# Low halves of the weights in three feed-forward stages: a negated copy and an adding transfer in place of a VectorE subtraction

## The chip, the cores and the metric

The kernel runs on one core of a Trainium2 chip. The metric is device time in microseconds of one execution. A core has TensorE (PE, matrix products into PSUM), VectorE (DVE), ScalarE (ACT), GpSimd (POOL) and SyncE (SP), which run side by side and wait for each other through semaphores, each through its own instructions in order. Sixteen DMA engines move data between memory (HBM) and the on-chip SBUF. Here SP issues the loads.

## What is computed

Two layers of a diffusion transformer on 256 latent and 256 context tokens of width 1024. Each layer is a half feed-forward step (FFN), a mixer (attention in the first layer, an mLSTM in the second) and another half FFN, each with a modulation and a layer norm:

```python
def half_ffn(h, shift, scale, gate, w_in, w_out, g, b):
    xm = modulate(h, shift, scale)
    a, u = jnp.split(xm @ w_in, 2, axis=-1)
    y = (jax.nn.silu(a) * u) @ w_out
    return post_norm(h, 0.5 * gate * y, g, b)

for i in range(DEPTH):
    mod_lat = split((silu(c) @ ada_w[i] + ada_b[i]), N_MOD)
    ...
    h_lat = half_ffn(h_lat, ..., ffn_w_in[i, 0], ffn_w_out[i, 0], ...)
    ...
    o_lat, o_ctx = attention_mixer(...)   # or mlstm_mixer
    ...
    h_lat = half_ffn(h_lat, ..., ffn_w_in[i, 1], ffn_w_out[i, 1], ...)
```

`w_in` is 1024 x 5632, `w_out` 2816 x 1024, all in float32. The result is `h_lat`. The last FFN sees the latent tokens alone.

## The kernel before

Every float32 matrix product is made of three products in a rounded format, float32r: an operand x is split into a high part h (x rounded) and a low part l = x - h, also rounded, and `mm3` (line 207) adds Wh·Xh, Wh·Xl and Wl·Xh in PSUM (lines 211, 214, 215). So each weight has to be loaded, rounded and subtracted before TensorE can use it. Weights come in blocks of 128 x 1024 (512 KB), eight 128 x 128 tiles each. One block feeds 24 matmuls.

The way of one block is `chunk` (line 187). `raw` issues the load from SP's queue into one of three raw buffers (tag "raw", `RAW = 3`). `pair` takes one of seven buffers (tag "w", `WB = 7`), each of which holds a high and a low part. `split` has ScalarE write the high part (line 194) and VectorE the low part (line 199). Once VectorE has read the raw buffer, SP may load into it again; once TensorE has used both parts, the pair is free. `fine` cuts VectorE's subtraction into four quarters around the layer norms, so that the norm's steps can go in between.

`ffn` is called three times (layer 0 before and after the attention, and layer 1 before the mLSTM; the first, second and third FFN below). Each goes over the hidden width in two halves of 11 units. A unit (`unit_in`) multiplies two blocks of `w_in` with the 512 tokens, takes the SiLU of one result on ScalarE, multiplies it with the other on VectorE and splits the product. `unit_out` then adds the half's part of `w_out`, eight columns from 11 blocks. In the second and third FFN the first four units (`LEAD`), and in all three the last four columns (`TAIL`), run once for the latent and once for the context tokens at half width, with their blocks kept, so that the layer norm of one group of tokens runs under the products of the other. The first FFN begins with `start`, which has its own loads and does the first four units with code of its own. `ffn_last`, the attention and the mLSTM use `chunk`, too.

Beside the weights each of the three FFNs loads blocks of `ada_w` (56, 40 and 32 of 512 KB, tag "ada", two buffers) through the same queue, two or three after each unit. VectorE takes two dot products of each (line 290).

In which order each engine's instructions stand is decided when the program is built, by a scheduler that follows the order of the code and its own estimate of when operands are ready; a few instructions are held in program order. In the layer norm (`norm`) POOL adds up three squares (line 417) and subtracts in four tiles (line 454).

Of the kernel before, what the change touches and what calls it, by code (L numbers as in the profile page):

```python
# [13 lines left out]
AF = mybir.ActivationFunctionType  # L14
ALU = mybir.AluOpType
# [96 lines left out]
class Stream:  # L112


    def __init__(self, b, chunks, sh=0):
        self.b, self.chunks, self.kept = b, chunks, (None, None)
        self.sh = sh if callable(sh) else lambda c: sh
# [24 lines left out]
class Body:  # L142
    def __init__(self, ctx, tc, a, out):
        self.tc, self.nc, self.a, self.out = tc, tc.nc, a, out
        self.n = 0
        self.sp = ctx.enter_context(tc.tile_pool(name="sp", bufs=1))
        self.pp = ctx.enter_context(tc.tile_pool(name="pp", bufs=1, space=PSUM))
        self.later, self.running = [], []
        self.fence = {}
        self.fine = False  # L150

        self.nraw, self.spare = 0, None

# [33 lines left out]
    def chunk(self, src, sh=0):  # L187
        r = self.raw(src)
        h, l = self.pair(sh=sh)
        self.split(r, h, l)  # L190
        return h, l

    def split(self, x, h, l):
# [331 lines left out]
    def ffn(self, layer, s, gate, groups, side, start=None):  # L525
        nc, V = self.nc, self.nc.vector
        li = layer * 2 + s
        allg = BOTH
        call = lambda *k: side.get(k, lambda: None)()
        with self.tc.tile_pool(name=f"ffn{li}", bufs=1) as gp:  # L530
            self.gp, self.gt, self.gw, self.gn = gp, {}, T, NFH
            done = 0
            if start:
                start(self)
                done = NSTART

            def unit_in(j, w, g, steps={}):
                n = g[1] - g[0]
                pa, pu = self.mm(), self.mm()
                for k in range(ND):  # L540
                    for part, o in ((0, pa), (1, pu)):
                        self.mm3(o[:, :n], w(k * 2 + part), self.x(k, g), k == 0, k == ND - 1)
                    self.steps(steps.get((j, k), ""))
                self.ffn_g(j, pa, pu, g)

            def unit_out(hf, d, w, g, steps={}):
                t0, t1 = g
                y = self.mm()
                for i in range(NFH):
                    gh, gl = self.gt[hf * NFH + i]  # L550
                    self.mm3(y[:, : t1 - t0], w(d * NFH + i), (gh[:, t0:t1], gl[:, t0:t1]), i == 0, i == NFH - 1)
                    self.steps(steps.get((int(g == CTX), d - (ND - TAIL), i), ""))
                for gg in groups:
                    if gg[0] >= t0 and gg[1] <= t1:
                        v = 0 if gg[0] == 0 else 1
                        z = self.h[:, d, gg[0] : gg[1]]
                        V.scalar_tensor_tensor(z, y[:, gg[0] - t0 : gg[1] - t0], gate()[:, v, d : d + 1], z, ALU.mult, ALU.add)  # L557
                        if hf:
                            self.add_sum(gg, d)

            w_in, w_out = self.a["ffn_in"][li], self.a["ffn_out"][li]
            stream = lambda j: Stream(self, [w_in[2 * j + i] for i in range(2)])
            for hf in range(2):
                js = list(range(hf * NFH, (hf + 1) * NFH))[0 if hf else done :]
                if hf == 0 and not start:
                    first = js[:LEAD]
                    ws = {j: Keep(self, [w_in[2 * j + i] for i in range(2)], SH) for j in first}
                    for g in groups:
                        assert len(self.running) == (g == LAT)
                        for j in first:  # L570
                            unit_in(j, ws[j], g, LEADSTEP if g == LAT else {})
                    for j in first:
                        call("in", j)
                    js = js[LEAD:]
                for j in js:
                    unit_in(j, stream(j), allg)
                    assert not self.running
                    if j >= LEAD + FAFTER:
                        self.fine = False
                    call("in", j)  # L580
                    self.residual(2)
                if not hf:
                    self.residual(len(self.later))
                w = Stream(self, [w_out[hf * NFH + i] for i in range(NFH)])
                body = ND - TAIL if hf else ND
                for d in range(body):
                    unit_out(hf, d, w, allg)
                    call("out", hf, d)
                if body < ND:
                    w = Keep(self, w.chunks, SH, w)  # L590
                    self.fine = True
                    for g in groups:
                        for d in range(body, ND):
                            unit_out(hf, d, w, g, TAILSTEP)
                    self.steps(ENDSTEP)


    def ffn_last(self, layer, gate):
# [800 lines left out]
```

## Time and profile before

| What | Value |
|---|---|
| Time of two runs | 1698.13 and 1702.44 us, median 1700.29 |
| Span of the profiled execution, from the first to the last instruction (its time, with what lies around the span, is not given apart from the two above) | 1693.6 us |
| Instructions | 24765 |
| q1, the queue of the loads | 71072 packets, 248.15 MB, 43.1% of 16 engines' span |
| Mean rate of all DMA | 148 GB/s |
| Loads of `ffn_in` / `ffn_out` / `ada_w`, 512 KB each | 168 / 66 / 139 |

A row of a group gives the line, the engine, the operation, the tile written and the tiles read with their shape, and the count; then the busy time and the mean of one in nanoseconds; then the idle time of the engine just before, and what ended it. A wait row gives who waited for whom: the total in microseconds, how often, and the longest. A row of the timeline begins with its start and its duration in microseconds. DMA share is the mean busy share of the 16 DMA engines. The lines themselves stand in the prediction, where they are used.

### The profile page before, as it was taken

The numbers are of one execution on the slowest core, as the hardware profiler recorded it, in microseconds if no ns is written. First come the engines' busy times: TensorE is split into PE (matmuls) and PEld (weight loads), VectorE is DVE, ScalarE is ACT, GpSimd is POOL, SyncE is SP. The second block draws the span as 40 slices with busy tenths as digits, with TensorE's granted clock in tenths as the row PEclk, the third lists the DMA queues.
The fourth block names the chain that finished last, engine by engine and source line by source line (L and its number), as shares of the span: only waits on it lengthen the run. The fifth ranks groups of instructions, "written<-read, shape, count | busy, mean of one in ns | idle before, by whom it ended". The sixth has DMA issues, their size and how long they took to land.

```text
span 1693.6 us, 24765 instructions
## 1 busy us (share of the span) xinstructions
PE 1643.8 (97%) x9432; PEld 1441.6 (85%) x9432; DVE 1231.7 (73%) x2681; ACT 656.3 (39%) x1125; POOL 93.6 (6%) x114
## 2 busy tenths in 40 slices
PE   7999999999899999999999999999999999999997
PEld 6888888899887898888888998888889878999986
DVE  6799977659988899996334977643335967998687
ACT  5622133215465452212331543213322645556541
POOL 0000000002321100000000100000001001120000
PEclk9999999999999999999999999999999999999999
DMA  9576765412102346774222257642221232337542
GB/s 356 184 230 231 236 210 199 149 62 77 61 2 82 119 136 234 229 244 152 93 94 75 101 179 247 215 144 98 99 100 63 94 125 76 113 125 246 178 168 94
DMA packets 71910, 250.49 MB, mean 148 GB/s; under 512 B 7920, under 2 KB 10480, under 8 KB 71792
## 3 DMA queue, kind: packets, MB, share of 16 engines
q1 hardware_dynamic: 71072, 248.15, 43.1%
q8 instruction: 74, 1.21, 0.3%
q10 hardware_dynamic: 720, 0.76, 0.1%
q14 instruction: 44, 0.36, 0.1%
HBM read 247.83 MB, written 1.05 MB: 147 GB/s over the span
## 4 chain that ended last, share of the span: by engine, by line
PE 83%; DVE 11%; ACT 3%; DMA 2%; issue 1%; POOL 0%; ACTq 0%; DVEq 0%; SPq 0%
PE t L214 23%; PE t L215 23%; PE t L211 23%; PE t L668 4%; DVE t L199 3%; PE t L1165 2%; PE t L726 2%; PE t L728 2%; PE t L727 2%; ACT t L194 1%; PE t L380 1%; DVE t L473 1%; DVE t L400 1%; DVE t L475 1%; DVE t L1201 1%
## 5 line engine op out<-in xcount | busy, mean ns | idle before, releaser
L211 PE MATMUL t<-t,t 128*128 128x512 f32 (+2 forms) x2540 | 856.1, 339 | 10.1 <-ACT t L194 7.5
L214 PE MATMUL t<-t,t 128*128 128x512 f32 (+2 forms) x2540 | 858.5, 339 | 1.8 <-DVE t L475 1.3
L215 PE MATMUL t<-t,t 128*128 128x512 f32 (+2 forms) x2540 | 854.4, 337 | 1.9 <-DVE t L199 1.9
L199 DVE TENSOR_TENSOR t<-t,t 128x256 fp32r<-128x256 f32 (+2 forms) x793 | 494.8, 659 | 196.4 <-ACT t L194 195.8
L194 ACT CAST t<-t 128x1024 fp32r<-128x1024 f32 (+2 forms) x463 | 397.7, 880 | 587.0 <-PE t L215 311.2
L211 PEld LDWEIGHTS t<-t,t 128*128 128x128 f32 x2540 | 476.6, 188 | 65.7 <-ACT t L194 9.8
L214 PEld LDWEIGHTS t<-t,t 128*128 128x128 f32 x2540 | 477.7, 188 | 56.5 <-DVE t L475 2.5
L215 PEld LDWEIGHTS t<-t,t 128*128 128x128 f32 x2540 | 477.5, 188 | 55.3 <-DVE t L199 2.8
L290 DVE SCALAR_TENSOR_TENSOR t<-t,t 128x1024 bf16<-128x1024 f32 x224 | 262.6, 1220 | 15.9 <-DMA t<-in_ada_w 15.4
L522 DVE TENSOR_TENSOR t<-t,t 128x512 f32<-128x512 f32 (+1 forms) x93 | 54.0, 585 | 112.1 <-PE t L215 92.4
L521 ACT ACTIVATE t<-t 128x512 f32<-128x512 f32 (+1 forms) x93 | 47.4, 515 | 196.9 <-PE t L215 195.0
L417 POOL TENSOR_TENSOR t<-t,t 128x256 f32<-128x256 f32 x30 | 23.3, 777 | 1161.4 <-ACT t L407 1159.9
L557 DVE SCALAR_TENSOR_TENSOR t<-t,t,t 128x256 f32<-128x256 f32 x96 | 42.7, 478 | 54.2 <-PE t L215 54.2
L726 PE MATMUL t<-t,t 128*128 128x256 f32 (+1 forms) x256 | 80.4, 316 | 0.0
L728 PE MATMUL t<-t,t 128*128 128x256 f32 (+1 forms) x256 | 79.7, 314 | 0.0
L727 PE MATMUL t<-t,t 128*128 128x256 f32 (+1 forms) x256 | 79.5, 313 | 0.0
L1165 PE MATMUL t<-t,t 128*128 128x512 f32 (+1 forms) x248 | 54.8, 373 | 11.0 <-ACT t L274 5.2
L1165 PEld LDWEIGHTS t<-t,t 128*128 128x128 f32 x248 | 46.4, 220 | 19.0 <-ACT t L274 5.2
L668 PE MATMUL t<-t,t 128*128 128x512 f32 x264 | 60.0, 389 | 0.0
L668 PEld LDWEIGHTS t<-t,t 128*128 128x128 f32 x264 | 49.5, 188 | 10.2
L407 ACT ACTIVATE t<-t 128x256 f32<-128x256 f32 x72 | 26.1, 413 | 68.3 <-DVE t L400 68.3
L726 PEld LDWEIGHTS t<-t,t 128*128 128x128 f32 x256 | 49.6, 194 | 3.1 <-DVE t L789 0.3
(164 smaller groups left out, 1067.6 us busy)
## 6 DMA issues: line engine op xcount, KB each, us to landing
t<-in_ffn_in SPq DMA_DIRECT2D x168, 512.0 KB, 4.0
t<-in_ada_w SPq DMA_DIRECT2D x139, 512.0 KB, 4.2
t<-in_ffn_out SPq DMA_DIRECT2D x66, 512.0 KB, 3.7
t<-in_ffn_last SPq DMA_DIRECT2D x22, 512.0 KB, 3.7
t<-in_att_in SPq DMA_DIRECT2D x12, 512.0 KB, 3.5
t<-in_att_out SPq DMA_DIRECT2D x8, 512.0 KB, 3.9
t<-in_ml_qk SPq DMA_DIRECT2D x8, 512.0 KB, 3.4
t<-in_ml_v SPq DMA_DIRECT2D x8, 512.0 KB, 4.0
```

Source lines behind the costliest of these rows:

```text
L194: self.behind(self.nc.scalar.copy(h, x))
L199: self.behind(self.nc.vector.tensor_tensor(out=ls, in0=xs, in1=hs.bitcast(F32), op=ALU.subtract))
L211: ins = mm(out, wh, xh, start=first, stop=False)
L214: mm(out, wh, xl, start=False, stop=False)
L215: mm(out, wl, xh, start=False, stop=last)
L290: ins = nc.vector.scalar_tensor_tensor(self.tmp().bitcast(BF16), r, 1.0, self.cb[:, v, :], ALU.mult, ALU.mult, accum_out=to)
L522: V.tensor_tensor(out=sl, in0=sl, in1=pu[:, :n], op=ALU.mult)
L668: pin(nc.tensor.matmul(ys[tt][i], gs[g], ws[k][w][:, i * 512 : (i + 1) * 512], start=k == 0 and g == w == 0, stop=k == NF - 1 and g == 1,))
L726: mm(o, self.xh[:, k, c], wh, start=k == 0, stop=False)
L727: mm(o, self.xh[:, k, c], wl, start=False, stop=False)
L728: mm(o, self.xl[:, k, c], wh, start=False, stop=k == ND - 1)
L1165: mm = lambda *k, **kw: pin(nc.tensor.matmul(*k, **kw))
```

## The change

While a flag is set, from the start of the FFN's units to its end, in each of the three FFNs, `chunk` no longer calls `split`. ScalarE writes the high part as before, and then the negative of the rounded block into the low part's place. A DMA that POOL issues adds the raw block onto it: l = -h + x. The subtraction on VectorE, and its quarters, are gone for these blocks. The loads, the products and the buffers are the same. The attention, the mLSTM, `start`, `ffn_last` and all splits of activations still use `split`.

```diff
@@ class Body, __init__
         self.fine = False
+        self.added = False
@@ def chunk
         r = self.raw(src)
         h, l = self.pair(sh=sh)
-        self.split(r, h, l)
+        if self.added:
+            S = self.nc.scalar
+            self.behind(S.copy(h, r))
+            self.behind(S.activation(l, r, AF.Copy, scale=-1.0))
+            self.nc.gpsimd.dma_start(l, r, accum_op=ALU.add)
+        else:
+            self.split(r, h, l)
         return h, l
@@ def ffn
                 start(self)
                 done = NSTART
 
+            self.added = True
+
             def unit_in(j, w, g, steps={}):
...
                     self.steps(ENDSTEP)
+            self.added = False
```

The lines move by up to ten: in the changed kernel the high part is line 193, the negated copy 194, the adding transfer 195, and `split`'s two steps are 201 and 206.

What moves, first on ScalarE in the units of the second half of the first FFN (128x1024 rows are weight blocks, 128x512 rows the SiLU and the split of its product). Before:

```order
L194 CAST t_1885<-t_1883 128x1024
L521 ACTIVATE t_1676<-t_1614 128x512
L194 CAST t_1935<-t_1933 128x1024
L194 CAST t_1674<-t_1676 128x512
L194 CAST t_1964<-t_1962 128x1024
L521 ACTIVATE t_1755<-t_1693 128x512
```

and now:

```order
L528 ACTIVATE t_1703<-t_1639 128x512
L193 CAST t_1968<-t_1966 128x1024
L201 CAST t_1701<-t_1703 128x512
L194 ACTIVATE t_1968<-t_1966 128x1024
L193 CAST t_1998<-t_1996 128x1024
L194 ACTIVATE t_1998<-t_1996 128x1024
L528 ACTIVATE t_1784<-t_1720 128x512
```

Each weight block now has two rows, and a unit's SiLU (line 528, before 521) stands behind four passes over blocks where there were two.

SP's queue in the second products of the first half of the first FFN (line 180 or 179: weights; 291 or 284: `ada_w`). Before:

```order
L179 DMA t_1171<-in_ffn_out 128x1024
L284 DMA t_810<-in_ada_w 128x1024
L179 DMA t_1200<-in_ffn_out 128x1024
L284 DMA t_817<-in_ada_w 128x1024
L284 DMA t_892<-in_ada_w 128x1024
```

and now:

```order
L180 DMA t_1185<-in_ffn_out 128x1024
L291 DMA t_816<-in_ada_w 128x1024
L180 DMA t_1215<-in_ffn_out 128x1024
L291 DMA t_823<-in_ada_w 128x1024
L291 DMA t_900<-in_ada_w 128x1024
```

The interleaving stays, three `ada_w` loads to two weight loads; what a weight load waits for is now the transfer of the third block before it.

POOL between the second and the third FFN (lines 417 and 454, now 424 and 461, are the layer norm's; `t_8769` and the later transfers belong to the third FFN's first units). Before:

```order
L417 TENSOR_TENSOR t_8392<-t_8387,t_8390 128x256
L417 TENSOR_TENSOR t_8392<-t_8392,t_8395 128x256
L417 TENSOR_TENSOR t_8392<-t_8392,t_8399 128x256
L454 TENSOR_TENSOR t_66<-t_66,t_8496 128x256 x4
L417 TENSOR_TENSOR t_8691<-t_8686,t_8689 128x256
```

and now:

```order
L195 DMA t_8769<-t_8767 128x1024
L424 TENSOR_TENSOR t_8446<-t_8441,t_8444 128x256
L424 TENSOR_TENSOR t_8446<-t_8446,t_8449 128x256
L424 TENSOR_TENSOR t_8446<-t_8446,t_8453 128x256
L195 DMA t_8799<-t_8797 128x1024
L195 DMA t_8859<-t_8857 128x1024
L461 TENSOR_TENSOR t_66<-t_66,t_8548 128x256 x4
L195 DMA t_8889<-t_8887 128x1024
```

POOL's queue in an FFN was empty up to the norm; now the norm's rows stand between the triggers of transfers, each of which waits for ScalarE.

## The prediction

> **What bounds the kernel now.** I read the page's head first, then a table of the span cut into stretches, then the groups of instructions by form, and then the waits of the DMA queue. The head says that TensorE is the busy engine:
>
> ```profile
> span 1693.6 us, 24765 instructions
> PE 1643.8 (97%) x9432; PEld 1441.6 (85%) x9432; DVE 1231.7 (73%) x2681; ACT 656.3 (39%) x1125; POOL 93.6 (6%) x114
> ```
>
> The stretches (PE, PEld, DVE, ACT, POOL busy, granted clock, share of the 16 DMA engines, GB/s) show where. 36 to 369 us is the first FFN behind its start, 610 to 928 the second, 965 to 1296 the third; the short ones are the passages between stages.
>
> ```profile
> core 0: us, PE busy (x) PEld busy (x) DVE busy (x) ACT busy (x) POOL busy (x), PEclk, DMA share, GB/s
> 0.00:36.00 36.00, 24.96 (x102) 21.53 (x103) 19.40 (x41) 17.48 (x33) 0.19 (x4) 1.00 0.95 370
> 36.00:100.00 64.00, 64.00 (x300) 53.48 (x299) 54.79 (x87) 35.09 (x58) 0.00 (x0) 1.00 0.61 200
> 100.00:200.00 100.00, 100.00 (x443) 82.81 (x442) 95.18 (x158) 25.09 (x28) 0.00 (x0) 1.00 0.72 238
> 200.00:300.00 100.00, 100.00 (x442) 82.79 (x442) 79.42 (x126) 28.13 (x35) 0.00 (x0) 1.00 0.59 203
> 300.00:369.00 69.00, 69.00 (x356) 59.24 (x355) 37.24 (x78) 14.73 (x17) 0.00 (x0) 1.00 0.34 115
> 369.00:402.00 33.00, 31.63 (x262) 30.99 (x262) 29.80 (x86) 14.89 (x31) 8.04 (x10) 1.00 0.18 59
> 570.00:610.00 40.00, 36.69 (x295) 35.18 (x295) 37.79 (x115) 18.10 (x42) 5.54 (x7) 1.00 0.16 54
> 610.00:850.00 240.00, 240.00 (x1148) 202.15 (x1148) 183.82 (x310) 72.79 (x97) 0.00 (x0) 1.00 0.56 186
> 850.00:928.00 78.00, 78.00 (x396) 66.69 (x395) 28.91 (x58) 17.09 (x20) 0.00 (x0) 1.00 0.25 88
> 928.00:965.00 37.00, 34.90 (x291) 34.07 (x291) 32.99 (x101) 15.54 (x31) 8.05 (x10) 1.00 0.26 92
> 965.00:1100.00 135.00, 135.00 (x737) 117.22 (x736) 96.09 (x186) 50.54 (x82) 0.00 (x0) 1.00 0.61 205
> 1100.00:1296.00 196.00, 196.00 (x917) 164.43 (x916) 74.83 (x115) 48.09 (x56) 0.00 (x0) 1.00 0.30 105
> 1296.00:1333.00 37.00, 35.21 (x292) 34.37 (x292) 33.83 (x104) 18.60 (x37) 8.05 (x10) 1.00 0.20 66
> ```
>
> Inside the three FFNs TensorE is busy in every microsecond. VectorE, from which work is taken, reaches 95.18 of 100 us and still nothing waits for it. So no VectorE time that is freed there can shorten the span. What can be gained lies in the four passages, where TensorE idles 1.37, 3.31, 2.10 and 1.79 us, 8.6 us in all. The reader should also see the DMA column: 0.61, 0.72, 0.59 in the first FFN. That is what the change adds to.
>
> TensorE's pace, from its timeline, at full and at half width of the moving tile:
>
> ```profile
> 65.64 0.39 PE L211 MATMUL t<-t,t 128*128 128x512 f32 x1
> 65.87 0.39 PE L214 MATMUL t<-t,t 128*128 128x512 f32 x1
> ```
>
> ```profile
> 937.75 0.28 PE L211 MATMUL t<-t,t 128*128 128x256 f32 x1
> 937.87 0.28 PE L214 MATMUL t<-t,t 128*128 128x256 f32 x1
> ```
>
> A weight block of 128x1024 feeds 24 matmuls: 24 x 0.227 = 5.44 us at full width, 24 x 0.118 = 2.83 us for one pass at half width (the first four units and the last four columns of an FFN). ScalarE's timeline shows the same beat, one block in 5.44 us, and the first block of the first FFN split at 58.07 us for a matmul at 65.64:
>
> ```profile
> 58.07 1.98 ACT L194 CAST t<-t 128x1024 fp32r<-128x1024 f32 x2
> 103.97 1.05 ACT L194 CAST t<-t 128x1024 fp32r<-128x1024 f32 x1
> 109.41 1.05 ACT L194 CAST t<-t 128x1024 fp32r<-128x1024 f32 x1 [3.34 <-PE t L215]
> ```
>
> **What the change removes and adds on the engines.** The prices per block:
>
> ```profile
> L194 ACT CAST t<-t 128x1024 fp32r<-128x1024 f32 x310 | 325.2, 1051 | 520.4 <-PE t L215 307.9 <-issue 139.8 <-DVE t L660 24.7
> L290 DVE SCALAR_TENSOR_TENSOR t<-t,t 128x1024 bf16<-128x1024 f32 x224 | 262.6, 1220 | 15.9 <-DMA t<-in_ada_w 15.4
> L199 DVE TENSOR_TENSOR t<-t,t 128x1024 fp32r<-128x1024 f32 x200 | 243.6, 1222 | 132.5 <-ACT t L194 132.3
> ```
>
> 190 blocks go through it: 36 + 44 + 44 of the first products, 22 in each of three second products. VectorE loses 190 x 1.22 = 232 us, all under a busy TensorE: 0 us of span in the bodies. ScalarE gains a second pass of the same size. No row shows a scaled copy of a whole block; the cast of the same shape is nearest, 1.05 us, so 190 x 1.05 = 200 us. Its share in 100:200 goes from 25 to 25 + 100 x 1.05/5.44 = 44%: hidden, too, and the SiLU behind it waits 1 us at most. In the passages VectorE's low parts stood among the steps of the layer norm; I give that 2 of the 8.6 idle us (bounds 0 and 8.6).
>
> **The transfer that adds.** It is the term that decides, and no row shows such a transfer. It moves 190 x 0.524 = 100 MB. Its engine time is bounded by loads. From the row 100:200: 0.72 x 100 us for 23.8 MB, 45.4 blocks, is 1.59 us of all 16 engines per block; from 0:36, where the engines are full, 0.95 x 36 us for 25.4 blocks is 1.35 us. The lower end is one full-rate load, 1.35 us; the upper end three loads at the dearer price (read the block, read the low tile, write it), 4.8 us. I take two full-rate loads, 2.7 us: with two operands the reading doubles while reading and writing go side by side, as in a load, and where it matters the engines are full as in 0:36. The page "Collectives: The Full Stack" of the Trainium skill, in "The bandwidth ceiling", puts the cost of an adding transfer in its two source reads and gives 62.28 against 32.35 GB/s; by that ratio of 1.93 a block would take 2.6 us and the sum below come to about 1745. No run here shows it yet.
>
> Now per stage, all loads at 1.35 us. The fullest row with the weights' three buffers and the two of `ada` is 0.72, the start's is 0.95; I let the engines fill to 0.92, nearer to the second, since here something is always queued.
> - First FFN, 36 to 369: 12.8 + 23.8 + 20.3 + 7.9 = 64.8 MB, 124 blocks, 167 us; 58 additions, 157 us; 324/0.92 = 352 us in a stretch of 333: +19. Its last block is due a half-width pass (44 x 3 x 0.118 = 15 us) before the end: +15. Nothing absorbs it, since TensorE takes the first block 7.6 us after its split begins, and no store of finished blocks exists yet. +34.
> - Second FFN, 610 to 850: 186 GB/s x 240 us is 85 blocks, 115 us; 44 additions, 119; 254 us after the fill: +14. In the last 78 us it fits. Up to six finished blocks (6 x 5.44 = 33 us) can stand ahead; the half-width passes at its head drain them, so I let half be absorbed: +7.
> - Third FFN, 965 to 1100: 53 blocks, 72 us; 25 additions, 68; 151 us: +16, half of it +8. Then 0.30 leaves room.
>
> **The three raw buffers.** The load of block n+3 waits until the raw buffer of block n is free:
>
> ```profile
> SPq L179 <- DVE t L199: 1105.5, 289, 84.6
> SPq L284 <- DVE t L290: 240.6, 120, 4.0
> ```
>
> Now it is freed by the adding transfer. SP is one queue in order, so the `ada` loads behind a waiting weight load wait as well, and VectorE's dot products with them. Landing times, in the window 100 to 200 us and over the whole run:
>
> ```profile
> t<-in_ffn_out SPq DMA_DIRECT2D x11, 512.0 KB, 4.6
> ```
>
> ```profile
> t<-in_ffn_in SPq DMA_DIRECT2D x168, 512.0 KB, 4.0
> ```
>
> One turn of a buffer is 4.6 (load) + 0.6 (ScalarE busy) + 2.1 (two passes) + L, and three turns' worth of TensorE is 3 x 5.44 = 16.3 us; so L, from ScalarE's end to the landing, may be 9.0 us. I estimate L as 2.7 + (4.0 - 1.35) + about 1.1 us for POOL to issue = 6.5 (bounds 4.0, a load's landing, and 12, two landings of 4.6 and three more): a turn of 13.8, 4.6 us per block. That holds 5.44 but not the 2.83 of the half-width passes. At the head of the second and the third FFN three loaded blocks are followed by three at 4.6: 3 x 1.8 = 5 us, of which some store is left; 4 us each, +8. POOL's layer-norm steps now stand behind such triggers:
>
> ```profile
> 941.88 3.45 POOL L454 TENSOR_TENSOR t<-t,t 128x256 f32<-128x256 f32 x4 [7.96 <-DVE t L449]
> ```
>
> POOL waits 7.96 us there for VectorE anyway, and triggers that stand ahead wait only for ScalarE: 0.
>
> **The sum:** 34 + 7 + 8 + 8 - 2 = +55 us on a span of 1693.6. The two timed runs lie 4.5 and 8.8 us over that span, their median 6.7; I add 55 to the median, 1700.3: 1755 us.
>
> **The rivals.**
> - *Hidden anyway (not slower).* If an addition costs the engines less than (318 x 0.92 - 167)/58 = 2.2 us, the first FFN fits too; at 1.35 us and L = 4.0 a turn is 11.3 of 16.3 us. Then only the passages speak: about 1698. For it: SBUF at both ends, no row at all against it. Against: two operands.
> - *A dear addition.* At 4.8 us: first FFN 167 + 278 = 445/0.92 = 484 + 15, +166; second (98 blocks, 58 additions) 132 + 278 = 410/0.92 = 446 against 318, +128; third (92 blocks, 61 additions) 124 + 293 = 417/0.92 = 453 against 331, +122; less two stores of 33, +6 of passages: about 2055. The steps between give 143 us for each us of price, so 1920 stands for 3.85 us.
> - *Latency, not rate.* If L exceeds 9.0 us though the engines have room (POOL slow to issue, or late to land), the three buffers set the pace: L = 12 makes 6.43 us per block, +0.99 x 177 blocks, less two stores of 33: about 1810. VectorE could do it by holding up POOL, each step of 1.22 us. The page "SBUF — State Buffer" of the Trainium skill, in "Who interferes with whom", has VectorE's two-input steps take only the read side of a port shared with POOL, while writing descriptors needs the write side; by that this cause falls away, and no run here shows it.
>
> **How the numbers follow.** Engines too full at about two loads per addition: 0.50 (own range 1720 to 1830). Hidden: 0.27. Dear: 0.13. Latency: 0.10. The prediction is the first one's, 1755. The range 1695 to 1920 takes in hidden and latency, and leaves out the dear case beyond 3.85 us and a little below, some 0.15. A measurement of this kernel tells about 2%, 34 us, from no change. Slower: 0.9 of the first, dear and latency, 0.66 with a little off for a short latency. Same: the rest of the first and nearly all of hidden, 0.32. Faster would take 34 us where 8.6 are idle: 0.02.
>
> **What would show it.** DVE's busy time near 1000 and ACT's near 855 us; POOL's transfers of 512 KB landing in about 6.5 us; a DMA share above 0.9 from 100 to 300 us; TensorE waiting at L222 (the third product, of low parts) for the adding transfer, mostly in the first FFN; SP's loads waiting for that transfer, no longer for VectorE. It is wrong if the share stays under 0.9 and TensorE still never idles (hidden), if the second and third FFN lose as much as the first (dear), or if blocks come late while the engines have room (latency).

## The result, and the profile after

The changed kernel takes 1778.31 us (median of 2 runs, 1775.22 to 1781.39), against 1700.29 before: a ratio of 1.0468, 95% interval 1.0440 to 1.0496. It is slower, by 78 us. The profiled execution took 1781.39 us; 86.0 us of span separate it from the one of before (1779.6 against 1693.6). That is 8 us more than the medians differ by. Where both are given, a time is 1.7 to 2.3 us above its span, so the profiled execution of before took an estimated 1695 to 1696 us, less than either of its timed runs, and the one of after is the slower of its two; the stage lengths below contain this spread.

The page's head and its strip of the DMA engines in 40 slices (9 is 90% busy or more), then its rows of queues (packets, MB, share of the time of all 16 engines):

```profile
span 1779.6 us, 25229 instructions
PE 1668.4 (94%) x9432; PEld 1457.6 (82%) x9432; DVE 1014.8 (57%) x2362; ACT 832.7 (47%) x1315; POOL 256.8 (14%) x304
...
DMA  9799999972201949999998559999987232255552
...
q1 hardware_dynamic: 71072, 248.15, 40.2%
q0 software_dynamic: 27360, 99.63, 30.3%
```

VectorE lost 217 us of work, ScalarE gained 176, and neither is what counts. TensorE runs the same 9432 matmuls and is busy 24.6 us longer: some of them ran at a lower clock. The queue q0 carries the 190 adding transfers: 0.303 x 1779.6 / 190 = 2.84 us of all 16 engines each. The 248.15 MB of q1 are 473 blocks of 512 KB: 0.402 x 1779.6 / 473 = 1.51 us for a load.

Where the span grew shows in POOL's timeline, where the first sum of a layer norm marks the end of each stage. Before (first FFN, attention, second FFN, third FFN):

```profile
372.24 2.46 POOL L417 TENSOR_TENSOR t<-t,t 128x256 f32<-128x256 f32 x3 [371.81 <-ACT t L407]
567.54 2.40 POOL L417 TENSOR_TENSOR t<-t,t 128x256 f32<-128x256 f32 x3 [42.73 <-ACT t L407]
...
931.23 0.76 POOL L417 TENSOR_TENSOR t<-t,t 128x256 f32<-128x256 f32 x1 [337.35 <-ACT t L407]
...
1299.11 2.46 POOL L417 TENSOR_TENSOR t<-t,t 128x256 f32<-128x256 f32 x3 [340.09 <-ACT t L407]
```

and after:

```profile
403.77 2.45 POOL L424 TENSOR_TENSOR t<-t,t 128x256 f32<-128x256 f32 x3 [19.42 <-ACT t L414]
598.32 2.40 POOL L424 TENSOR_TENSOR t<-t,t 128x256 f32<-128x256 f32 x3 [3.96 <-ACT t L414]
989.23 2.45 POOL L424 TENSOR_TENSOR t<-t,t 128x256 f32<-128x256 f32 x3 [14.88 <-ACT t L414]
1384.88 2.45 POOL L424 TENSOR_TENSOR t<-t,t 128x256 f32<-128x256 f32 x3 [20.32 <-ACT t L414]
```

So the first FFN is 31.5 us longer, the attention 0.8 shorter, the second FFN 27.2 and the third 27.8 longer, and all behind them is unchanged: 31.5 - 0.8 + 27.2 + 27.8 = 85.7 of the 86.0. The three stages that the diff touches lose nearly alike, which the prediction didn't expect.

A table by stage (columns as in the prediction's) divides this further. Before:

```profile
66.00:372.20 306.20, 306.20 (x1414) 256.08 (x1413) 242.28 (x405) 84.47 (x103) 0.00 (x0) 1.00 0.57 192
567.50:931.20 363.70, 360.39 (x1883) 309.61 (x1882) 255.28 (x495) 111.63 (x166) 7.78 (x10) 1.00 0.44 148
931.20:1299.10 367.90, 365.80 (x1940) 315.61 (x1940) 203.84 (x399) 114.18 (x169) 8.05 (x10) 1.00 0.41 141
```

and after:

```profile
66.00:403.80 337.80, 312.62 (x1419) 258.86 (x1418) 180.25 (x335) 136.41 (x161) 48.16 (x57) 0.96 0.96 265
598.30:989.20 390.90, 367.34 (x1882) 314.39 (x1881) 183.34 (x380) 172.10 (x230) 62.38 (x74) 0.97 0.88 228
989.20:1384.90 395.70, 375.23 (x1941) 322.58 (x1940) 128.14 (x280) 174.91 (x234) 63.35 (x76) 0.97 0.85 217
```

Two things are to be seen. TensorE idles 25.2, 23.6 and 20.5 us in the three stages, where it idled 0, 3.3 and 2.1; and its busy time for the same work grew by 6.4, 7.0 and 9.4. And the DMA share, 0.57, 0.44 and 0.41 before, is 0.96, 0.88 and 0.85. In the first FFN 0.96 x 337.8 = 324 us of engine time stand against 306 us of matmuls: no order of the loads within the stage can hide that, as long as each takes this engine time. In the second and third it is 344 and 336 us, against 364 and 368 of before: over the whole stage it would fit.

What TensorE waits for (sum, times, longest), and what SP's queue, ScalarE and VectorE wait for:

```profile
PE t L218 <- ACT t L201: 44.4, 12, 11.2
PE t L218 <- DVE t L529: 15.7, 3, 8.6
...
PE t L222 <- DMA t<-t: 2.5, 2, 1.2
```

```profile
ACT t L193 <- DMA t<-in_ffn_in: 254.8, 86, 7.3
DVE t L297 <- DMA t<-in_ada_w: 194.3, 79, 9.4
...
ACT t L193 <- DMA t<-in_ffn_out: 105.1, 33, 5.8
```

```profile
SPq L180 <- DMA t<-t: 729.6, 175, 26.1
```

VectorE's row for `in_ada_w` was 15.4 us before. SP's loads of weights now wait for the adding transfer, and since SP issues in order, the `ada_w` loads behind them wait as well. TensorE hardly waits for the adding transfer itself (L222, 2.5 us). It waits at the first of the three products for L201, ScalarE's cast of a gate product, or for L529, VectorE's gate product.

These are few waits, and long ones. Seven of the twelve for L201, 7.5 us, stood in the kernel before as well. Of the five others the two longest come in the first FFN, three matmuls apart, where the second products begin and need the last gate products:

```profile
167.05 0.80 PE L218 MATMUL t<-t,t 128*128 128x512 f32 x1 [10.77 <-ACT t L201]
...
180.21 0.80 PE L218 MATMUL t<-t,t 128*128 128x512 f32 x1 [11.21 <-ACT t L201]
```

The waits for L529 differ in kind. The longest ends at 710.72 us, just after VectorE's gate product (709.98 + 0.68 = 710.66) and before the end of that product's cast, which ScalarE runs from 710.70 to 711.32. So this matmul does not read the gate product. By the code it waits for one of the six accumulators (tag "mm"), which the gate product had still to read.

The second wait of the first FFN, followed back through the timelines of ScalarE and VectorE:

```profile
179.54 0.62 ACT L201 CAST t<-t 128x512 fp32r<-128x512 f32 x1 [7.69 <-DVE t L529]
```

```profile
176.53 1.23 DVE L297 SCALAR_TENSOR_TENSOR t<-t,t 128x1024 bf16<-128x1024 f32 x1 [3.65 <-DMA t<-in_ada_w]
...
177.68 1.22 DVE L297 SCALAR_TENSOR_TENSOR t<-t,t 128x1024 bf16<-128x1024 f32 x1
...
178.82 0.68 DVE L529 TENSOR_TENSOR t<-t,t 128x512 f32<-128x512 f32 x1
```

Read from the bottom: a block of `ada_w` lands late, VectorE stands at its two dot products, the gate product is written behind them, ScalarE stands at the cast of that gate product, and TensorE idles 11.21 us. All three engines work in the order written. This looks like a clear story, the dot products holding up VectorE; the experiments below show that it is only one of the ways in which the same lateness comes through.

### The profile page after: what moved, and what is told of

The parts are those of the page before. It is cut to its first block, busy times and chain, and to the rows that moved or that the text cites. A ratio compares the mean times of both kernels' runs of the same rounds, so it can differ in the third digit from the quotient of the medians.

```text
span 1779.6 us, 25229 instructions
## 1 busy us (share of the span) xinstructions
PE 1668.4 (94%) x9432; PEld 1457.6 (82%) x9432; DVE 1014.8 (57%) x2362; ACT 832.7 (47%) x1315; POOL 256.8 (14%) x304
## 3 DMA queue, kind: packets, MB, share of 16 engines
q1 hardware_dynamic: 71072, 248.15, 40.2%
HBM read 247.83 MB, written 1.05 MB: 140 GB/s over the span
## 4 chain that ended last, share of the span: by engine, by line
PE 55%; DMA 21%; DVE 13%; issue 7%; ACT 4%; POOL 0%; SPq 0%; DVEq 0%; ACTq 0%; POOLq 0%
PE t L218 15%; PE t L221 15%; PE t L222 15%; DMA t<-t 8%; DMA t<-in_ada_w 4%; DMA t<-in_ffn_in 4%; PE t L678 3%; DMA t<-in_ffn_out 3%; DVE t L206 3%; DVE t L297 2%; PE t L1175 2%; ACT t L201 1%; PE t L736 1%; PE t L738 1%; PE t L737 1%
## 5 line engine op out<-in xcount | busy, mean ns | idle before, releaser
L218 PE MATMUL t<-t,t 128*128 128x512 f32 (+2 forms) x2540 | 865.4, 342 | 67.4 <-ACT t L201 44.4
L221 PE MATMUL t<-t,t 128*128 128x512 f32 (+2 forms) x2540 | 866.6, 342 | 1.8 <-DVE t L482 1.2
L222 PE MATMUL t<-t,t 128*128 128x512 f32 (+2 forms) x2540 | 861.1, 340 | 4.0 <-DMA t<-t 2.5
L218 PEld LDWEIGHTS t<-t,t 128*128 128x128 f32 x2540 | 481.6, 190 | 127.6 <-ACT t L201 49.0
L221 PEld LDWEIGHTS t<-t,t 128*128 128x128 f32 x2540 | 482.6, 190 | 58.9 <-DVE t L206 2.5
L222 PEld LDWEIGHTS t<-t,t 128*128 128x128 f32 x2540 | 482.5, 190 | 58.7 <-DMA t<-t 2.8
L193 ACT CAST t<-t 128x1024 fp32r<-128x1024 f32 x190 | 199.4, 1049 | 432.5 <-DMA t<-in_ffn_in 254.8
L206 DVE TENSOR_TENSOR t<-t,t 128x256 fp32r<-128x256 f32 (+3 forms) x474 | 255.9, 570 | 158.3 <-ACT t L201 157.3
L201 ACT CAST t<-t 128x1024 fp32r<-128x1024 f32 (+2 forms) x273 | 203.2, 759 | 226.5 <-DVE t L529 102.2
L195 POOL DMA_DIRECT2D t<-t x190 | 163.7, 861 | 987.3 <-ACT t L194 780.1
L194 ACT ACTIVATE t<-t 128x1024 fp32r<-128x1024 f32 x190 | 200.3, 1054 | 0.0
L529 DVE TENSOR_TENSOR t<-t,t 128x512 f32<-128x512 f32 (+1 forms) x93 | 53.9, 584 | 225.1 <-ACT t L528 129.8
L1175 PEld LDWEIGHTS t<-t,t 128*128 128x128 f32 x248 | 47.5, 225 | 19.1 <-ACT t L281 5.0
L678 PEld LDWEIGHTS t<-t,t 128*128 128x128 f32 x264 | 49.5, 188 | 10.2
```

The costliest lines, as they stand in the source:

```text
L193: self.behind(S.copy(h, r))
L194: self.behind(S.activation(l, r, AF.Copy, scale=-1.0))
L195: self.nc.gpsimd.dma_start(l, r, accum_op=ALU.add)
L201: self.behind(self.nc.scalar.copy(h, x))
L206: self.behind(self.nc.vector.tensor_tensor(out=ls, in0=xs, in1=hs.bitcast(F32), op=ALU.subtract))
L218: ins = mm(out, wh, xh, start=first, stop=False)
```

## The experiments

Two theories stood after this profile. **Engine time**: the 16 DMA engines are asked for more than they have, an adding transfer costing two loads, so loads of both kinds land late. **Order**: the engines would do, but VectorE's dot products stand in front of the gate products, so that a late `ada_w` block costs more than it should. A third, **latency**, was the three raw buffers' turn. Each kernel below is the changed one with one edit. "Before" ran beside them, 1698.89, 1698.79 and 1698.36 us in three groups, and ratios are to it. The stage lengths are from the same marks of POOL as above:

| kernel | us | first FFN's end | second FFN | third FFN |
|---|---|---|---|---|
| before | 1700.3 | 372.2 | 363.7 | 367.9 |
| the change | 1778.3 | 403.8 | 390.9 | 395.7 |
| VectorE adds | 1698.3 | 372.7 | 365.7 | 368.6 |
| plain copy | 1719.2 | 384.0 | 372.3 | 369.6 |
| one `ada_w` block | 1711.9 | 372.1 | 367.0 | 378.0 |
| the same, four raw buffers | 1706.4 | 372.8 | 366.9 | 376.2 |
| dots apart | 1795.7 | 417.9 | 396.4 | 393.4 |
| every second block | 1709.8 | 378.7 | 373.1 | 367.8 |
| late blocks only | 1698.4 | 372.6 | 365.9 | 368.8 |
| fewer loads a place | 1770.8 | 399.5 | 391.2 | 388.4 |
| dots a place later | 1775.2 | 404.5 | 384.3 | 396.5 |
| even loads | 1751.4 | 403.0 | 374.8 | 379.5 |
| even, and dots later | 1753.5 | 403.3 | 373.6 | 379.7 |

**ScalarE's second pass alone.** VectorE adds the block onto its negative high part; no transfer.

```diff
-            self.nc.gpsimd.dma_start(l, r, accum_op=ALU.add)
+            self.behind(self.nc.vector.tensor_tensor(out=l, in0=r, in1=l.bitcast(F32), op=ALU.add))
```

> The second ScalarE pass stays (negated rounded block), but VectorE adds the raw block onto it in one 1.22 us step, with no transfer on POOL. R: no more than before, 1698 to 1708. L: same as before, 1698 to 1708. A (ScalarE's second pass is the cause): 1750 to 1780.

1698.29 us, ratio 0.9997 (0.9988 to 1.0007), with ScalarE busy 837.5 us. The 190 added passes of 1.05 us cost nothing that can be measured, so the loss belongs to the transfer and to what waits for it.

**A plain copy in place of the addition**.

```diff
-            self.nc.gpsimd.dma_start(l, r, accum_op=ALU.add)
+            self.nc.gpsimd.dma_start(l, r)
```

> Leaves out: the addition in the transfer; it only copies the raw block over the low part, so the products are not the reference's. Same queue, same waits, same 512 KB written. R with two reads as the cost: engine time per transfer falls from 2.84 to about 1.4 to 1.6 us, the first FFN needs 167 + 58 x 1.5 = 254 us of engines in 318, time 1698 to 1715. If the addition costs nothing beyond a copy: 2.8 us and 1770 to 1785. L: landing falls by 1.4 of 6.9 us only, 1755 or more. A: 1770 to 1780.

1719.19 us, 1.0125 (1.0108 to 1.0142), 4 us above what was expected. Its queue row:

```profile
q0 software_dynamic: 27360, 99.63, 16.2%
```

0.162 x 1714.7 / 190 = 1.46 us for a copy of the same bytes by the same queue. The addition takes 2.84 / 1.46 = 1.94 times that, about the two loads that the prediction took. The Trainium skill's page "Collectives: The Full Stack" gives a ratio of 1.93 in "The bandwidth ceiling", and this run agrees. With the same transfers, the same triggers and the same waits at half the engine time, 59 of the 78 us are gone. The landing falls with it, from 6.9 to 4.7 us (median), so this run alone does not part the two. 20 us stay: 11.8 in the first FFN and 8.6 in the second.

**One block of `ada_w` for each FFN**, loaded once and used for all its dot products (the other loads are left out; of 139 in the whole kernel 14 stay).

```diff
-        r = self.t([P, 1024], tag="ada", bufs=2, pool=self.gp)
-        self.nc.sync.dma_start(r, self.a["ada_w"][layer, dt])
-        return r
+        if self.kept_ada[0] is not self.gp:
+            r = self.t([P, 1024], tag="ada", bufs=2, pool=self.gp)
+            self.nc.sync.dma_start(r, self.a["ada_w"][layer, dt])
+            self.kept_ada = (self.gp, r)
+        return self.kept_ada[1]
```

> Leaves out: all loads of ada_w in the three FFNs but one each, whose block serves all dot products, so the modulation is not the reference's. Everything else is the changed kernel. Theory R (the 16 DMA engines are full; the ada_w loads come late, VectorE stands in order at their dot products, the gated products behind them come late, TensorE waits): 192 fewer blocks than capacity asks, engines near 0.75 of full, time 1695 to 1708. Rival L (the way of one block through load, two ScalarE passes and the added transfer with three raw buffers is too long even with free engines): 1765 to 1780. Rival A (the second ScalarE pass in order holds up SiLU and split): 1770 to 1780.

1711.88 us, 1.0075 (1.0060 to 1.0090). The first FFN is back at 372.1, with all its additions at about the same price, 0.318 x 1708.9 / 190 = 2.86 us:

```profile
q0 software_dynamic: 27360, 99.63, 31.8%
```

Its fullest stretch:

```profile
100.00:200.00 100.00, 100.00 (x443) 82.84 (x442) 80.99 (x153) 46.56 (x53) 18.07 (x21) 1.00 0.92 216
```

and the same stretch of the changed kernel:

```profile
100.00:200.00 100.00, 76.75 (x320) 61.58 (x319) 59.55 (x107) 36.46 (x43) 12.90 (x15) 0.86 1.00 277
```

At a share of 0.92 TensorE never idles; at 1.00 it idles 23 of 100 us. So the price of an addition is not the trouble by itself, but an addition together with the `ada_w` loads.

It is not the full engines alone either. In the next stretch of the changed kernel the share is 1.00 as well, and TensorE never idles; no second products begin in it:

```profile
200.00:300.00 100.00, 100.00 (x443) 82.79 (x442) 61.24 (x113) 38.40 (x44) 14.61 (x17) 1.00 1.00 290
```

And the plain copy (first row) and this run (second row) ask for the same engine time in the first FFN, 0.83 x 318.0 = 264 and 0.86 x 306.1 = 263 us. One loses 11.8 us there, the other nothing:

```profile
66.00:384.00 318.00, 309.51 (x1414) 257.95 (x1412) 179.38 (x334) 136.45 (x158) 29.69 (x57) 0.98 0.83 280
66.00:372.10 306.10, 306.10 (x1413) 256.10 (x1412) 177.57 (x334) 136.69 (x158) 48.18 (x57) 1.00 0.86 199
```

So below full engines it counts whether late `ada_w` loads stand in the queues at all. Some 13 us stay, 4 more than the upper end expected, 10.1 of them in the third FFN.

**The same with a fourth raw buffer** in the three FFNs (`ada` gets one buffer, the room goes to a raw one).

```diff
+            r = self.t([P, 1024], tag="ada", bufs=1, pool=self.gp)
...
-            self.added = True
+            self.added, self.spare = True, gp
...
-            self.added = False
+            self.added, self.spare = False, None
```

> Leaves out: as in the run with one block of ada_w for each FFN. Beside it a fourth raw buffer in the three FFNs, in the place of the second ada buffer. What is left there, 13 us, came at the heads of the second and the third FFN. If it is the turn of three raw buffers in half-width passes: a turn of 13.8 us over four buffers is 3.5 us per block where 2.83 is asked, 1700 to 1706. If it is the length of the way of the first blocks or POOL's order: 1709 to 1714.

1706.42 us, 1.0046 (1.0032 to 1.0059), 5.5 us less, and just above the 1700 to 1706 expected of the buffers' turn. But the profiles do not place the gain at the heads. Of the 5.8 us between the two spans (1708.9 and 1703.1) the second FFN has 0.1 and the third 1.8; 3.5 lie behind the third FFN, where neither kernel uses the fourth buffer. So of the 13 us 1.9 at most can be put down to the buffers' turn, and what the others are stays open.

**The dot products taken off the loads.** The loads of `ada_w` stay, but the dot products read the conditioning vectors, so VectorE never waits for a load.

```diff
-            self.tmp().bitcast(BF16), r, 1.0, self.cb[:, v, :], ALU.mult, ALU.mult, accum_out=to
+            self.tmp().bitcast(BF16), self.cb[:, 1 - v, :], 0.001, self.cb[:, v, :], ALU.mult, ALU.mult, accum_out=to
```

> Leaves out: the data of ada_w in the dot products (they read the conditioning vectors instead, so the modulation is not the reference's). All loads of ada_w stay on SP's queue with their bytes, all dot products stay on VectorE, but no dot product waits for a load. R in its first form (loss goes through VectorE standing in order at late ada_w blocks): at most 1725, TensorE's waits for ScalarE's casts of gated products gone. R in its second form (weights themselves late because the engines are full): 1755 to 1785, TensorE waiting for the added transfer. L and A: 1770 to 1780.

1795.70 us, 1.0573 (1.0556 to 1.0590), slower still, and outside what either form of the theory gave. The loads are also no longer held back by VectorE, so they crowd the engines earlier; this is not the change with the waits alone removed. But it shows where the lateness goes when VectorE is free. TensorE's longest wait, ScalarE ahead of it, and VectorE ahead of that:

```profile
184.31 0.79 PE L218 MATMUL t<-t,t 128*128 128x512 f32 x1 [13.17 <-ACT t L201]
```

```profile
182.69 1.04 ACT L193 CAST t<-t 128x1024 fp32r<-128x1024 f32 x1 [6.59 <-DMA t<-in_ffn_out]
183.64 0.61 ACT L201 CAST t<-t 128x512 fp32r<-128x512 f32 x1
```

```profile
176.13 0.69 DVE L529 TENSOR_TENSOR t<-t,t 128x512 f32<-128x512 f32 x1 [0.86 <-ACT t L528]
```

VectorE had the gate product ready at 176.8, but its cast stands on ScalarE behind the high part of a weight block that has not landed. The wait ends at the same line, for the same kind of cast, by another late load.

**Every second block added**, the others split by VectorE as before.

```diff
-        self.added = False
+        self.added, self.nadd = False, 0
...
-        if self.added:
+        self.nadd += 1
+        if self.added and self.nadd % 2:
```

> Only every second weight block of the three FFNs goes the new way, the other one is split as before. Theory R (TensorE loses time only where the DMA engines have more to do than time allows): by the engine times of the changed kernel, 1.43 us a load and 2.97 an addition, the first FFN asks 124 x 1.43 + 29 x 2.97 = 263 us of 333, the first 240 us of the second 85 x 1.43 + 22 x 2.97 = 187: nothing is over full, 1697 to 1710. If the loss goes with the number of additions: half of 78, 1735 to 1742.

1709.81 us, 1.0064 (1.0050 to 1.0078). Half of the transfers cost 11 us, not half of 78: the cost is far from proportional. It does not start only at full engines, though: the first FFN loses 6.5 us and the second 9.4, where by the sums of the expectation nothing was over full.

**Late blocks only**: 66 of the 190, those of the second half of the second and third FFN, where the `ada_w` loads run out.

```diff
-            self.added = True
-
...
             for hf in range(2):
+                self.added = bool(hf and li)
                 js = list(range(hf * NFH, (hf + 1) * NFH))[0 if hf else done :]
```

> The new way only in the second half of the hidden width of the second and the third FFN, 66 blocks; elsewhere split as before. R: in the second FFN some ada_w loads still run beside it, 0.5 + 2.97/5.44 = 1.05 of the engines for a while; in the third 0.30 + 0.55 = 0.85: 1697 to 1706. No gain over the kernel before beyond 0.2%. If the loss goes with the number of additions: 1700 + 78 x 66/190 = 1727.

1698.43 us, 0.9996 (0.9987 to 1.0005). A third of the work moved where the engines have room costs nothing. It also gains nothing, since VectorE, which it relieves, was never waited for.

**Fewer loads at a place.** The `ada_w` loads are handed out over more places, the remainder always rounded up, so that the second FFN's first ten places still get two each.

```diff
+        left = [26 if len(ada) > 40 else 30]
+
         def pop():
-            for _ in range(3 if len(ada) > 40 else 2):
-                if ada:
-                    b.ada(*ada.pop(0))
+            left[0] -= 1
+            for _ in range(math.ceil(len(ada) / (left[0] + 1)) if ada else 0):
+                b.ada(*ada.pop(0))
```

> The changed kernel with the loads of ada_w of each FFN spread over all its units and columns (30 places instead of 20 and 16 in the second and the third; in the first 26 as before). R: the first FFN loses its 31 us as before; the second asks 98 x 1.43 + 58 x 2.97 = 312 of 318 us, the third 92 x 1.43 + 61 x 2.97 = 313 of 331, so their losses of 27 and 28 fall to 5 to 18 each: 1735 to 1765. If the additions' own way is what costs: 1775 or more.

1770.75 us, 1.0413 (1.0397 to 1.0430): some 8 us, and less than expected. The second FFN, whose first places were unchanged, stays at 391.2; the third gains 7, the first 4. Two more runs went after this, one for each theory.

**Dots a place later**: the loads stay where they were, but the dot products of the last two are written at the next place, about 11 us of TensorE later.

```diff
+        wait = []
+
         def pop():
-            for _ in range(3 if len(ada) > 40 else 2):
-                if ada:
-                    b.ada(*ada.pop(0))
+            n = min(3 if len(ada) > 40 else 2, len(ada))
+            for r, layer, dt, vecs in wait:
+                for v in vecs:
+                    b.ada_dot(r, layer, dt, v)
+            wait.clear()
+            for i in range(n):
+                layer, dt, vecs = ada.pop(0)
+                if i < n - 2:
+                    b.ada(layer, dt, vecs)
+                else:
+                    wait.append((b.ada_load(layer, dt), layer, dt, vecs))
```

> The ada_w loads keep their places, but the dot products of the last two loads of a place are written at the next place, some 10 us of TensorE later, so VectorE no longer stands in front of a gate product for a load that has just been issued. In the second and third FFN (two loads to a place) that takes away all of VectorE's waiting in front of a gate product; in the first (three to a place) one load in three is still waited for at once. If the loss in the second and third FFN goes through VectorE's dot products, the two stages fall from 391 and 396 us to 370 to 380, and the time to 1735 to 1755. If the engines are simply too full and the weight blocks are late by themselves, the two stages stay at 385 to 396 and the time at 1765 to 1785.

1775.22 us, 1.0451 (1.0425 to 1.0478). The third FFN is as long as in the change (396.5), the second 6.6 us shorter. VectorE still waits for `ada_w` there, in the third FFN 53.8 us, against 57.5 in the change (the second row):

```profile
DVE t L297 <- DMA t<-in_ada_w: 53.8, 20, 7.4
```

```profile
DVE t L297 <- DMA t<-in_ada_w: 57.5, 18, 8.1
```

The use stands about 11 us later, a load lands 6.7 us after its issue (median of this run), and it still is not there. So it was issued late: SP's queue, which is worked in order, stands 729.0 us before weight loads that wait for the adding transfer (729.6 in the change). The loads are late by what SP and the engines do ahead of them, not by where their use is written; this run does not part the two.

**Even loads**: the same number over all places (56 over 26 in the first FFN, 40 and 32 over 30), the dot products where the change has them.

```diff
+        at = [0, len(ada), 26 if len(ada) > 40 else 30]
+
         def pop():
-            for _ in range(3 if len(ada) > 40 else 2):
-                if ada:
-                    b.ada(*ada.pop(0))
+            k, m, n = at
+            at[0] += 1
+            for _ in range((k + 1) * m // n - k * m // n if ada else 0):
+                b.ada(*ada.pop(0))
```

> The ada_w loads are spread evenly over the places of an FFN (in the first FFN 56 over 26, in the second 40 and the third 32 over 30), with the dot products where they were. The second and the third FFN use 0.88 and 0.85 of the engines over 391 and 396 us, 344 and 336 us, which fits into the 364 and 368 us of before if it is even. Engine time alone: second and third stage 370 to 382 us, first as in the run with fewer loads to a place (399), time 1735 to 1755. If two late loads at a place are enough to hold the engines in order, however evenly they lie: 1755 to 1775.

1751.42 us, 1.0310 (1.0291 to 1.0328). The second and third FFN give back 16 us each, 16.1 of 27.2 and 16.2 of 27.8; the first, whose 324 us of engine time exceed its 306 us of matmuls, gives back 0.8. That is what the sums of the section above called for. In the first FFN the loss moves and does not shrink: TensorE's longest waits there are now 9.37 us at 166.59 and 9.34 us at 362.11, one at the start of the second products of each half, where the change has both at the first.

**Both.**

> Both of the other two together: loads evenly spread, dot products a place later. If both the fullness at one time and the order of the dot products matter, it is the best of the three: 1715 to 1745. If the order of the dot products is worth nothing, it equals the even one within 6 us; if the spread is worth nothing, it equals the one with the dot products a place later within 6 us.

Here the loads go over 25 and 29 places, since the last place takes dot products alone. 1753.53 us, 1.0325 (1.0300 to 1.0351), the same as even loads alone, within their spread. The place of the dot products is worth nothing that these runs can tell.

No version beats the kernel before: the two that equal it are the one without transfers and the one with a third of them.

## Why the prediction was right, and where its steps were not

**The direction and the cause** were right: slower, by DMA engines too full at about two loads per addition. The time came out 23 us above the forecast of 1755, inside its range. One of the prediction's signs misled: "if the second and third FFN lose as much as the first (dear)". They lose 27.2 and 27.8 us against 31.5, nearly as much, at a price far from the dear one's.

**The price.** 2.7 us was taken and 2.84 measured; 1.35 for a load, against 1.51 over the run. The rival with a hidden addition needed less than 2.2 us, the dear one 3.85 and more: both fall by the row of q0. Latency as the rival had it, with engines that have room, does not fit shares of 0.96, 0.88 and 0.85. The landing was estimated at 6.5 us from ScalarE's end, and its median is 6.9 from the issue, under the limit of 9.0 (the longest is 12.1); POOL's issuing, put at about 1.1 us, took 0.86. From the view of line 195, durations (shortest, median, longest) and landings:

```profile
L195 POOL DMA_DIRECT2D t<-t x190: 850/859/1010, 62.5 to 1363.7; - x190
```

```profile
DMA to landing us min/median/max: 4.4/6.9/12.1
```

No trigger took more than 1.01 us, and the only wait for VectorE before one was 3.7 us. That agrees with what the prediction cited from the Trainium skill's page "SBUF — State Buffer", "Who interferes with whom".

**The first FFN**: +34 forecast, +31.5 measured, but not by the steps that were added up, so that the closeness is in part luck. The sum had weight blocks late, with TensorE waiting at L222, 15 of the 34 us for the half-width pass at the end. Measured are 25.2 us of idle time and 6.4 of slower matmuls, a term the sum did not have; 22.0 of the idle time are the two waits for gate products at 167 and 180 us, and from 300 us to the end TensorE idles only 1.9. With all `ada_w` loads but one left out its loss is gone, and with the addition at half price it is 12 us.

**The second and third FFN**: this is where the sum was mis-sized, +11 and +12 with their heads, against +27.2 and +27.8. The step that failed is "I let half be absorbed", by up to six finished blocks ahead of TensorE. A store of finished weight blocks covers late blocks; TensorE was stopped by late gate products, for which no store exists; once they came it went through L221 and L222 without waiting. The waits at L218 and the near absence of waits at L222 say so, and the two chains (through VectorE in the change, through ScalarE with the dots apart) say how. That gate products were late, and finished weights hardly ever (2.5 us at L222), is shown; that the store of finished blocks is the reason for the second is argued. Without the absorption, and with 2.84 us for an addition and 1.43 for a load (53.0 us for the 37 blocks of this row from 100 to 200 us),

```profile
q1 hardware_dynamic: 5330, 19.41, 53.0%
```

the prediction's own lines give (85 x 1.43 + 44 x 2.84)/0.92 - 240 = 28 and (53 x 1.43 + 25 x 2.84)/0.92 - 135 = 25 us. That is an estimate after the fact, without the heads and the clock; that it comes near the measured 27.2 and 27.8 proves no step of it.

**The clock** was not in the sum at all. 22.8 us of the three stages' 86.5 are a longer busy time for the same matmuls, 6.4, 7.0 and 9.4 by stage, at a granted clock of 0.96, 0.97 and 0.97 where it was 1.00.

**The heads.** The turn of a raw buffer was put at 4.6 us a block and costs 4.5; ScalarE's timeline at the head of the second FFN has each high part waiting for its load:

```profile
604.17 1.05 ACT L193 CAST t<-t 128x1024 fp32r<-128x1024 f32 x1 [2.28 <-DMA t<-in_ffn_in]
...
608.72 1.05 ACT L193 CAST t<-t 128x1024 fp32r<-128x1024 f32 x1 [2.54 <-DMA t<-in_ffn_in]
```

A third one stands at 613.17, and a step of the modulation (L481) behind it: TensorE waits 4.44 us for it at 614.68, where it waited 2.56 before. Four microseconds for each of two heads were forecast. Without the `ada_w` loads the second FFN is 3.3 us longer and the third 10.1.

At the third FFN's head the largest wait is another one. The prediction looked for the layer norm's steps behind triggers on POOL and put that at nothing; they stood behind weight blocks on ScalarE. In the run with one `ada_w` block (there the high part is line 194, the squares line 417):

```profile
961.28 1.05 ACT L194 CAST t<-t 128x1024 fp32r<-128x1024 f32 x1 [5.03 <-PE t L223]
...
963.19 1.32 ACT L417 ACTIVATE t<-t 128x256 f32<-128x256 f32 x4
```

```profile
968.07 1.87 PE L390 MATMUL t<-t,t 128*128 128x1 f32 x8 [5.25 <-DVE t L427]
```

The norm's squares (L417) start at 963.19, after both passes over a block that had to wait 5.03 us for its pair of buffers, and the matmul that needs their sum waits 5.25 us. Before, the squares began at 955.10 and that matmul waited 0.60 us; in the changed kernel it waits 3.85. With a fourth raw buffer the squares stand ahead of the block, in another order, and the wait is 1.13.

**The passages' gain of 2 us** cannot be told from nothing: the version with a third of the blocks is the kernel before within 0.1%. ScalarE's second pass was costed at nothing, rightly where no transfer stands behind it (1698.29 us); what it does at the third head is told above.

**What was looked for in the profile**: VectorE near 1000 (1014.8), ScalarE near 855 (832.7), a share above 0.9 from 100 to 300 us, SP's loads waiting for the transfer, all seen. The wait at L222 was wrong, as said, and "mostly in the first FFN" with it.

**Open** stay the rest of the heads, and the 11 us that the second and the third FFN each still lose with even loads. How the loss divides between lateness through VectorE and through ScalarE was not measured; moving the one left the other. Nor was it measured how much of the lateness is engine time and how much SP's order, with `ada_w` loads behind weight loads that wait for the transfer: no run gave the changed kernel more raw buffers with its `ada_w` loads in place.

## What to carry to other kernels

Before moving arithmetic from an engine into a transfer, sum the DMA engines' time by stage, an SBUF-to-SBUF addition counting two copies, and compare it with the stage's matmuls. Here even places gave back 16 of 27 us in stages where it fitted, and 0.8 of 31.5 where it did not; fitting alone was no safety, as the plain copy and every second block show. Don't count a store of prefetched operands as cover when the late loads also feed other engines that work in order: look for what those engines produce, since that is what the matmul will wait for. And an engine that nothing waits for, even at 95% busy, is not worth relieving.

## What the runs showed beside it

After an idle time of 11.21 us TensorE's matmuls came at half pace for some 5.5 microseconds:

```profile
180.21 0.80 PE L218 MATMUL t<-t,t 128*128 128x512 f32 x1 [11.21 <-ACT t L201]
...
181.95 0.63 PE L218 MATMUL t<-t,t 128*128 128x512 f32 x1
182.38 0.63 PE L221 MATMUL t<-t,t 128*128 128x512 f32 x1
...
185.72 0.40 PE L218 MATMUL t<-t,t 128*128 128x512 f32 x1
185.96 0.39 PE L221 MATMUL t<-t,t 128*128 128x512 f32 x1
```

From start to start it is 0.43 us up to 185.4, and 0.23 from there. Twelve matmuls from 180.21 took 5.5 us where 12 x 0.227 = 2.7 are the pace, so an idle time of 11 us cost 2.8 us more than itself; the granted clock of the stretch from 150 to 200 us, with two such waits, was 0.73:

```profile
150.00:200.00 50.00, 28.01 (x106) 21.56 (x105) 33.49 (x59) 18.23 (x21) 6.02 (x7) 0.73 0.99 274
```

The Trainium skill's page "TensorE: Matmul & The Clock Gate", in "Part 1: The HAM clock gate", describes such a fall of the clock after an idle window and a return after a few microseconds of work; the rows agree.
